# Latent attention with its transposes in groups of eight, and four sets of loads issued at other places

## The chip, the core and the metric

The kernel runs on one core of a Trainium2 chip. A core has five engines that run side by side, each working through its own instructions in the order in which they were written: TensorE (PE in the profile, its weight loads PEld), VectorE (DVE), ScalarE (ACT), GpSimd (POOL) and SyncE (SP), which here issues all the DMAs. They wait for one another through semaphores. Matrix products are written to PSUM, eight banks of 512 float32 columns on 128 partitions; everything else lies in SBUF. The metric is the device time in microseconds of one execution.

## The reference

One layer of an encoder for 1024 tokens of width 1024: a normalisation, one combined input projection, two attention branches, each multiplied by SiLU of its own projection z and projected back, a gated sum of the two, an output projection, the residual and a last normalisation.

```python
proj = h @ w_in          # split into c_q, c_kv, k_rope, z_mla, q/k/v_dil, z_dil, g_mla, g_dil
a_out = mla_attention(c_q, c_kv, k_rope, ...)      # 8 heads, dense softmax over 1024 keys
y_mla = (a_out * silu(z_mla)) @ w_o_mla
d_out = dilated_mixture(q_dil, k_dil, v_dil, positions)   # 3 groups of 8 heads, mixed by softmax denominators
y_dil = (d_out * silu(z_dil)) @ w_o_dil
merged = sigmoid(g_mla + b) * y_mla + sigmoid(g_dil + b) * y_dil
out = rmsnorm(x + merged @ w_out)
```

In one head of the latent attention (`mla_attention`): `s = q @ k.T`, `p = softmax(s)`, `out = p @ v`, with 96 columns of q and k and 64 of v.

## The kernel before, in words

**Precision.** A float32 operand is split into a high part of reduced precision (fp32r, a copy by ScalarE) and a low part (the difference, by VectorE or GpSimd); a product is then three matrix products, high-high, high-low and low-high (`mm3`, lines 145 to 147; `split`, lines 151 and 152). Almost all of the work of TensorE comes from these three lines.

**Order.** The program is written out in full, and each engine executes in the order in which the lines are reached; nothing is reordered. The stages are: the latents and the values of the dilated attention (`first_products`, `first_stage`, to about 205 us), the q and k of the dilated attention and four gates by a scheme with fewer block products (`blocks`), the dilated attention (`attention`), the latent attention (`mla_attention`, about 797 to 1085 us) and the output (`output`). During both attentions a generator, `self.fill`, hands out pieces of another projection whenever `feed` is called: first `gate_fill` (SiLU and gate projections), later `proj_fill` (the two projections back, with the gates).

**The value chunks.** `first_stage` runs 48 chunks `c`, 16 for each of three groups `g` (`r` is the place in the group); a chunk is twelve products of one token tile with one half of the value weights (`v_part`). The weights of a half are loaded by `v_load` in four DMAs into two raw tiles of a pool with two buffers (`w_raw`), and split by `v_split` into four pairs `w_h`, `w_l`: those of the first half of the next group in chunks r = 12 to 14, those of its second half in r = 0 to 2 of that group. The chunks with r = 4 to 7 are the first that use the second half. `block_sums` is a generator whose steps are called once per chunk from c = 30 on, at the end of the chunk: step 1 issues twelve loads (`y`), step 3 scales the first four tiles on ScalarE (line 571), step 4 starts four sums on GpSimd (lines 575 to 578), and later steps split those sums (`parts`, `s_h` on ScalarE and `s_l` on VectorE). `self.table` loads four cosine and sine pieces (`cs_d`) for the stage `blocks`.

**A unit of latent attention.** A unit `k` is one head and two blocks of 128 queries; 32 units run one after another, four ticks `c` each (`mla_tick`). The softmaxed scores P of a unit (128 queries by 1024 keys, twice) have to be transposed for the product with the values: sixteen transposes, four to a tick, written to one of two PSUM banks called `pt` in turn (`mla_transposes`, line 1063). ScalarE copies such a bank to a high part (line 1065), VectorE subtracts to get the low part (`mla_low`, line 1071), and four products with the values follow (`mla_values`, lines 1087 and 1088). They add up in a bank `m_av`, of which there is one; an even unit fills its left half, the odd unit after it the right half. When both are through, in tick 0 of the next even unit, ScalarE copies one part (`mla_copied`, line 1094) and VectorE adds the other (`mla_sum`, line 1103). In ticks 0 and 1 of unit k the scores of unit k + 1 are computed (`mla_scores`), their maxima are taken by VectorE (`mla_maxima`, line 1047) and their exponentials by ScalarE (line 1055). In ticks 2 and 3 `feed` is called. After the last unit of a pair of heads in one half of the queries, `mla_spread` transposes the softmax denominators (line 1117), also into a `pt` bank, and VectorE takes reciprocals (lines 1119, 1120).

The banks and the one accumulator are set here:

```python
b = self.banks
self.places.update(pt=b[0:2], pj=b[2:4], m_av=[])
...
self.places["pj"], self.places["m_av"] = [b[i]], [b[1 - i]]
```

**Loads beside it.** The end of the dilated attention (`combine`, pair 3) is spread over the first ticks of the latent attention: `spread` loads shares of the mixture, `weighted` multiplies by them (line 1636); step 9 comes in tick 15, step 10 in tick 17, step 11 in tick 19. `proj_fill` loads three gate tiles when it begins (tick 34), and its jobs use them in line 1003.

Of the kernel before, what the change touches and what calls it, by code (L numbers as in the profile page):

```python
# [11 lines left out]
F32R = mybir.dt.float32r  # L12
# [37 lines left out]
ZG = (4, 5, 6, 7, 0, 1, 2, 3, *range(16, 24))  # L50
# [11 lines left out]
class Net:  # L62
# [540 lines left out]
    def first_stage(self, cp, dpool, sums):  # L603

        tc, nc = self.tc, self.nc
        self.v_raw, self.v_w, self.v_ps, self.blk, self.opd = {}, {}, {}, {}, {}
        with ExitStack() as ctx, ExitStack() as left, ExitStack() as inner:
            pool = lambda stack, name, bufs=1, **k: stack.enter_context(tc.tile_pool(name=name, reuse_waits="tile", bufs=bufs, **k))
            pl = pool(ctx, "pj_l", 4, space=PSUM)
            pj = pool(ctx, "pj_a", 4, space=PSUM)  # L610
            vp = pool(ctx, "dvp", 3, side="right")
            lp = pool(left, "lp")
            with ExitStack() as stack:
                wl, xp = pool(stack, "wl"), pool(stack, "xp", 3)
                self.first_products(lp, wl, xp, (pj, pl))
            mpool, up, tp = pool(left, "cosm"), pool(left, "up"), pool(left, "lt", 2)
            self.cos_m, self.sin_m = self.table(mpool, "cs_m", 32)
            weights = self.up_weights(up, tp)
            latents = self.latents(next(weights), up, tp, pl)
            self.latent_factors(tp)  # L620
            m = self.masks
            self.mask0 = m[:, 64:320], m[:, 384:640], m[:, 640:896]
            self.mask1 = m[:, 128:384], m[:, 0:256]
            steps, later = 0.0, None
            for c in range(48):
                self.v_part(c, pj, vp)
                g, r = divmod(c, 16)
                if 2 <= c < 10:
                    self.latent_scaled(c - 2)
                if 5 <= c < 8:  # L630
                    next(weights)
                if c == 20:
                    self.token_row(tp, pl)
                first, second = (0, 1) if g & 1 else (1, 0)
                if r == 6:
                    self.v_load(g + 1, first)
                if r == 14:
                    self.v_load(g + 1, second)
                if g < 2 and 12 <= r < 15:
                    for i in ((0, 1), (2,), (3,))[r - 12]:  # L640
                        self.v_split(first, i, nc.gpsimd if g == 0 else nc.vector)
                if g and r < 3:
                    for i in ((0, 1), (2,), (3,))[r]:
                        self.v_split(1 - (g & 1), i, nc.gpsimd if g == 1 else nc.vector)
                if c == 29:
                    self.cos_d, self.sin_d = self.table(dpool, "cs_d", 0)
                if c == 35:
                    self.block_loads(0, self.block_items[0], (self.wp, None))
                if c >= LATENTS_BEGIN and latents:
                    steps += LATENTS_PACE  # L650
                    while steps >= 1 and latents:
                        steps -= 1
                        try:
                            next(latents)
                        except StopIteration:
                            latents = None
                            left.close()
                            sp = pool(sums, "sums")
                            z = self.zero = sp.tile([128, 512], F32, name="zero")
                            nc.gpsimd.memset(z, 0.0)  # L660
                            later = self.block_sums(sp, pool(inner, "bs"))
                elif later and c >= 30:
                    next(later, None)
                if c >= 44:
                    for j in ((0, 1), (2,), (3,), (4,))[c - 44]:
                        self.block_minus(j, self.block_items)
                        self.block_operand(j, self.block_items, nc.vector)
            run_all(later)
            self.block_minus(LEAD, self.block_items)
# [241 lines left out]
    def gate_fill(self):  # L911

        nc = self.nc

        def after(job, i, half, ps):

            z = self.get("zg_g" if 16 <= job < WIDE_END else "zg_z")
            t = self.get("zg_t") if i < 8 else z
            c = slice(half * 512, half * 512 + 512)
            dst = self.zs[i][:, c] if i < 8 else self.gt[i - 8][:, c]  # L920
            yield nc.vector.tensor_tensor(out=z, in0=ps, in1=self.R[:, c], op=ALU.mult)
            if i < 8:
                yield nc.scalar.activation(out=t, in_=z, func=AF.Tanh, scale=0.5)
                nc.gpsimd.tensor_tensor(out=t, in0=t, in1=z, op=ALU.mult)
                nc.gpsimd.tensor_tensor(out=t, in0=t, in1=z, op=ALU.add)
            else:
                yield nc.scalar.activation(out=t, in_=z, func=AF.Tanh, scale=0.5, bias=self.hb[:, i - 8:i - 7])
            stores.append((dst, t))

        def store():  # L930
            if stores:
                self.dma(*stores.pop(0))
        stores = []
        tail = iter(())
        for n, i in enumerate(ZG):
            w = self.split_weights.pop(n)
            for half in range(2):
                next(tail, None)
                ps = self.get("pj")
                t = slice(half * 512, half * 512 + 512)  # L940
                for kc in range(8):
                    self.mm3(ps, *self.at(w, kc), self.hTh[:, kc, t], self.hTl[:, kc, t], kc == 0, kc == 7)
                    if half == 0 and kc == 0:
                        self.weights_load(n + 2)
                    if half == 0 and kc == 4:
                        self.weights_split(n + 1)
                    if kc == 2 or kc == 5 and self.one_bank:
                        store()
                    if kc % 2 and kc < 7:
                        next(tail, None)  # L950
                    if kc < 7:
                        yield
                run_all(tail)
                tail = after(2 * n + half, i, half, ps)
                if self.one_bank:
                    next(tail)
                yield True
        store()
        run_all(tail)
        store()  # L960
        store()

    def proj_fill(self):
# [6 lines left out]
        def gate(n):  # L970
            if n < len(jobs):
                i, dt, half = jobs[n]
                t = self.get("gate")
                self.dma(t, self.gt[8 * i + dt][:, 512 * half:512 * half + 512])
                return t
# [3 lines left out]
        k, pair = 0, (1, 0)  # L979
        for n, (i, dt, half) in enumerate(jobs):  # L980
            while not (self.brd_done if i else self.brm_done[half]):
                yield
            if pair != (i, dt // 2):
                tile, k, pair = tile + 1, 0, (i, dt // 2)
# [72 lines left out]
    def mla_transposes(self, k, c):  # L1057

        pt = self.get("pt")
        for c2 in range(2):  # L1060
            for b in range(2):
                kc, o = 2 * c + c2, c2 * 256 + b * 128
                self.nc.tensor.transpose(pt[:, o:o + 128], self.P[k, b][:, 128 * kc:128 * kc + 128], self.ident)  # L1063
        h, l = self.get("pt_h", dtype=F32R), self.get("pt_l", dtype=F32R)
        self.nc.scalar.copy(out=h, in_=pt)  # L1065
        self.pt[k, c] = pt, h, l

# [82 lines left out]

    def mla_tick(self, k, c):

        self.mla_transposes(k, c)
        if c == 0:
            self.mla_low(k, c)
            self.mla_scores(k + 1, 0)
            self.mla_values(k - 1, 3)
            self.mla_copied(k - 1)
            self.mla_spread(k)
            self.mla_maxima(k + 1, 0)  # L1160
            self.mla_sum(k - 1)
            h, u = self.units[k - 1] if k else (0, 0)
            if u == 3 and h < 6:
                self.mla_load_v(h + 2)
        elif c == 1:
# [7 lines left out]
            if u == 3 and h < 6:  # L1173
                self.mla_load_qk(h + 2)
        else:
            if c == 2:
                self.mla_exponentials(k + 1, 1)
            self.mla_low(k, c)
            self.feed(self.rate)
            self.mla_values(k, c - 1)  # L1180
            if c == 2:
                for n in {6: (), 7: (), 8: (5,), 9: (7,)}.get(k, (k - 1,)):
                    self.mla_merged(n, self.nc.gpsimd)
# [373 lines left out]
    def combine(self, pair, st, nums):  # L1557
# [82 lines left out]
            p.tensor_tensor(out=nums[0][:, c], in0=nums[0][:, c], in1=nums[g][:, c], op=ALU.add)  # L1640

        def step9():
            for half in range(2):
                weighted(0, half, v)
                add(1, half)
            self.turn["bc"] = 1

        def step10():
            spread(2, 0, halves[1])
            weighted(2, 0, v)  # L1650
            add(2, 0)
            self.turn["bc"] = 4
# [247 lines left out]
```

## Time and profile before

| what | us |
|---|---|
| median of 3 runs | 1215.23 (1213.33 to 1217.88) |
| the profiled execution | 1215.87 |
| its span, first to last instruction | 1214.1 |
| TensorE busy in it | 1197.5 |
| VectorE, ScalarE, GpSimd busy | 739.8, 606.1, 557.5 |

The mean granted clock of TensorE was 0.996 of full speed. The 1.8 us between the time of the execution and its span lie before the first and after the last instruction. A busy share close to 100% on TensorE does not mean that each product ran at its best pace, since the products overlap; how far apart two products start is the better measure. In the rows of the timeline the first number is the start, the second the duration, then engine, line, operation, tiles written and read, shapes and count; idle time before it and what ended it stand in brackets. Names such as `at_r` and `at_f` are places in SBUF that many tiles share; `bank`, `left` and `right` are PSUM banks.

### The profile page before, as it was taken

Reading aid. Unit: us, or ns where it says so; the run is one execution under the profiler, and the core shown is the slowest. Engines: PE = TensorE matmul, PEld = TensorE weight load, DVE = VectorE, ACT = ScalarE, POOL = GpSimd, SP = SyncE. Lnnn points to the kernel's source line nnn. Section 1 sums busy time; section 2 is a strip of 40 time slices with the busy share of each in tenths; the row PEclk is TensorE's granted clock in tenths of the full one; section 3 lists DMA queues with packets and bytes.
Section 4 is the critical chain, followed back from the end, with each engine's and each line's share of the span. In section 5 each row is a group of like instructions: output and inputs, shape, how many; then the busy total and the mean of one; then the engine's idle time right before and its main releaser. Section 6 shows DMA issues by size and latency. Waiting matters only on the chain.

```text
span 1214.1 us, 18210 instructions
## 1 busy us (share of the span) xinstructions
PE 1197.5 (99%) x6343; PEld 1030.1 (85%) x6343; DVE 739.8 (61%) x1289; ACT 606.1 (50%) x1259; POOL 557.5 (46%) x473
## 2 busy tenths in 40 slices
PE   9999999999999999999999999999999999999997
PEld 8888878888888888889889899888888888888886
DVE  6775447466666653345666666566757767669442
ACT  6633346343434435356565657454655656654222
POOL 1413027877777777544374624335820111258322
PEclk9999999999999999999999999999999999999999
DMA  8757983597355642397899898937462534235141
GB/s 282 227 192 267 330 311 108 195 281 194 106 139 153 177 122 108 101 289 212 239 258 274 247 263 245 260 107 188 137 171 78 139 105 123 79 121 181 74 154 52
DMA packets 128924, 221.30 MB, mean 182 GB/s; under 512 B 28024, under 2 KB 66496, under 8 KB 123904
## 3 DMA queue, kind: packets, MB, share of 16 engines
q1 hardware_dynamic: 128832, 220.14, 60.5%
q8 instruction: 50, 0.82, 0.3%
q14 instruction: 42, 0.34, 0.1%
HBM read 149.24 MB, written 70.85 MB: 181 GB/s over the span
## 4 chain that ended last, share of the span: by engine, by line
PE 89%; DMA 5%; POOL 2%; DVE 1%; ACT 1%; issue 1%; SPq 0%; POOLq 0%; ACTq 0%; DVEq 0%
PE bank L145 7%; PE bank L146 7%; PE bank L147 7%; PE pj L146 5%; PE pj L147 5%; PE pj L145 5%; PE bank L1063 4%; PE st_d L146 2%; PE st_a L146 2%; PE st_c L146 2%; PE st_c L147 2%; PE st_a L147 2%; PE st_d L147 2%; PE st_d L145 2%; PE st_a L145 2%; PE st_c L145 2%
## 5 line engine op out<-in xcount | busy, mean ns | idle before, releaser
L152 POOL TENSOR_TENSOR w_l<-w_raw,w_h 128x512 fp32r<-128x512 f32 x175 | 230.1, 1327 | 213.2 <-ACT w_h L151 164.5
L151 ACT CAST w_h<-w_raw 128x512 fp32r<-128x512 f32 x188 | 111.7, 620 | 121.7 <-POOL w_raw L684 98.1
L145 PE MATMUL bank<-at_r,w_h 128*128 128x512 f32 x344 | 141.6, 412 | 0.0
L146 PE MATMUL bank<-at_r,w_h 128*128 128x512 f32 x344 | 135.4, 394 | 0.5 <-POOL at_r L152 0.5
L147 PE MATMUL bank<-at_r,w_l 128*128 128x512 f32 x344 | 135.5, 394 | 0.0
L1071 DVE TENSOR_TENSOR at_r<-bank,at_r 128x512 fp32r<-128x512 f32 x128 | 87.9, 687 | 69.0 <-ACT at_r L1065 68.5
L1065 ACT CAST at_r<-bank 128x512 fp32r<-128x512 f32 x128 | 74.9, 585 | 85.4 <-PE bank L1063 84.8
L684 POOL TENSOR_TENSOR w_raw<-w_raw 128x512 f32<-128x512 f32 x64 | 83.2, 1300 | 6.3 <-DVE w_l L152 5.6
L1063 PE MATMUL bank<-consts,at_f 128*128 128x128 f32 x512 | 76.9, 272 | 0.5 <-DVE at_r L1071 0.5
L147 PEld LDWEIGHTS bank<-at_r,w_l 128*128 128x128 f32 x344 | 64.8, 188 | 14.5
L146 PE MATMUL pj<-w_l,at_r 128*128 128x512 f32 x192 | 75.5, 393 | 1.2 <-DVE w_l L152 1.2
L145 PE MATMUL pj<-w_h,at_r 128*128 128x512 f32 x192 | 75.7, 394 | 0.7 <-ACT w_h L151 0.7
L1336 DVE TENSOR_TENSOR at_r<-bank,at_r 128x512 fp32r<-128x512 f32 x64 | 43.9, 685 | 53.0 <-ACT at_r L1332 52.7
L147 PE MATMUL pj<-w_h,at_r 128*128 128x512 f32 x192 | 75.4, 392 | 0.0
L146 PEld LDWEIGHTS bank<-at_r,w_h 128*128 128x128 f32 x344 | 65.2, 189 | 9.7 <-POOL at_r L152 1.0
L145 PEld LDWEIGHTS bank<-at_r,w_h 128*128 128x128 f32 x344 | 65.0, 189 | 8.9
L1088 PE MATMUL bank<-at_r,at_r 128*128 128x256 f32 x256 | 67.2, 284 | 4.2 <-DVE at_r L1071 4.2
L1087 PE MATMUL bank<-at_r,at_r 128*128 128x256 f32 x256 | 67.2, 283 | 0.0
L1317 ACT ACTIVATE at_f<-at_f,at_f 128x256 f32<-128x256 f32 x128 | 64.1, 505 | 1.4 <-DVE at_f L1310 1.4
L1332 ACT CAST at_r<-bank 128x512 fp32r<-128x512 f32 x64 | 37.5, 586 | 54.3 <-PE bank L1324 53.1
L1063 PEld LDWEIGHTS bank<-consts,at_f 128*128 128x128 f32 x512 | 59.3, 140 | 1.3 <-DVE at_r L1071 0.9
L1088 PEld LDWEIGHTS bank<-at_r,at_r 128*128 128x128 f32 x256 | 48.7, 190 | 10.2 <-DVE at_r L1071 5.1
(335 smaller groups left out, 3287.1 us busy)
## 6 DMA issues: line engine op xcount, KB each, us to landing
w_raw<-wt SPq DMA_DIRECT2D x48, 512.0 KB, 4.0
at_r<-s_dq SPq DMA_DIRECT2D x32, 512.0 KB, 8.0
s_dk<-dq_st SPq DMA_DIRECT2D x80, 128.0 KB, 2.3
s_dv<-dv_st SPq DMA_DIRECT2D x16, 512.0 KB, 3.4
s_dq<-dq_st SPq DMA_DIRECT2D x64, 128.0 KB, 2.4
zt<-s_gt SPq DMA_DIRECT2D x32, 256.0 KB, 3.8
w_raw<-wv SPq DMA_DIRECT2D x24, 256.0 KB, 5.7
at_r<-s_dk SPq DMA_DIRECT2D x8, 576.0 KB, 11.8
```

Of the source, the lines that this page charges most:

```text
L145: mm(out, lh, rh, start=start, stop=False, skip_group_check=skip)
L146: mm(out, lh, rl, start=False, stop=False, skip_group_check=skip)
L147: return mm(out, ll, rh, start=False, stop=stop, skip_group_check=skip)
L151: self.nc.scalar.copy(out=h, in_=raw)
L152: sub.tensor_tensor(out=l, in0=raw, in1=h.bitcast(F32), op=ALU.subtract)
L684: self.nc.gpsimd.tensor_tensor(out=b[out], in0=b[x], in1=b[y], op=ALU.subtract)
L1063: self.nc.tensor.transpose(pt[:, o:o + 128], self.P[k, b][:, 128 * kc:128 * kc + 128], self.ident)
L1065: self.nc.scalar.copy(out=h, in_=pt)
L1071: self.nc.vector.tensor_tensor(out=l, in0=pt, in1=h.bitcast(F32), op=ALU.subtract)
L1087: mm(out, vv[:, kc], ph[:, x], start=kc == 0, stop=False)
L1088: mm(out, vv[:, kc], pl[:, x], start=False, stop=kc == 7)
L1317: nc.scalar.activation(out=p, in_=p, func=AF.Exp, scale=-1.0, bias=nm, accum_out=den)
```

## The change

Four things are edited. `mla_transposes` no longer copies; a new function `mla_high` does. Transposes are issued in pairs of groups, eight in a row, in ticks 0 and 2, and the order of copies, low parts, value products and scores within a unit changes with it. The generator of the sums is called from c = 29 on and at the head of a chunk's remaining work, ahead of the loads and splits of value weights; the second half of the last group's value weights is loaded at r = 11 and not at 14, the cosine table at c = 33 and not at 29. The first gate tile of `proj_fill` is loaded by the last job of `gate_fill`. The last share of pair 3 is loaded at the head of step 9 and not in step 10.

```diff
--- before.py
+++ after.py
@@ -632,9 +632,11 @@
                 if c == 20:
                     self.token_row(tp, pl)
                 first, second = (0, 1) if g & 1 else (1, 0)
+                if later and c >= 29:
+                    next(later, None)
                 if r == 6:
                     self.v_load(g + 1, first)
-                if r == 14:
+                if r == (11 if g == 1 else 14):
                     self.v_load(g + 1, second)
                 if g < 2 and 12 <= r < 15:
                     for i in ((0, 1), (2,), (3,))[r - 12]:
@@ -642,7 +644,7 @@
                 if g and r < 3:
                     for i in ((0, 1), (2,), (3,))[r]:
                         self.v_split(1 - (g & 1), i, nc.gpsimd if g == 1 else nc.vector)
-                if c == 29:
+                if c == 33:
                     self.cos_d, self.sin_d = self.table(dpool, "cs_d", 0)
                 if c == 35:
                     self.block_loads(0, self.block_items[0], (self.wp, None))
@@ -659,8 +661,6 @@
                             z = self.zero = sp.tile([128, 512], F32, name="zero")
                             nc.gpsimd.memset(z, 0.0)
                             later = self.block_sums(sp, pool(inner, "bs"))
-                elif later and c >= 30:
-                    next(later, None)
                 if c >= 44:
                     for j in ((0, 1), (2,), (3,), (4,))[c - 44]:
                         self.block_minus(j, self.block_items)
@@ -946,6 +946,9 @@
                         self.weights_split(n + 1)
                     if kc == 2 or kc == 5 and self.one_bank:
                         store()
+                    if kc == 5 and n == len(ZG) - 1 and half:
+                        self.first_gate = self.get("gate")
+                        self.dma(self.first_gate, self.gt[8][:, 0:512])
                     if kc % 2 and kc < 7:
                         next(tail, None)
                     if kc < 7:
@@ -970,6 +973,8 @@
         def gate(n):
             if n < len(jobs):
                 i, dt, half = jobs[n]
+                if n == 0:
+                    return self.first_gate
                 t = self.get("gate")
                 self.dma(t, self.gt[8 * i + dt][:, 512 * half:512 * half + 512])
                 return t
@@ -1061,7 +1066,11 @@
             for b in range(2):
                 kc, o = 2 * c + c2, c2 * 256 + b * 128
                 self.nc.tensor.transpose(pt[:, o:o + 128], self.P[k, b][:, 128 * kc:128 * kc + 128], self.ident)
-        h, l = self.get("pt_h", dtype=F32R), self.get("pt_l", dtype=F32R)
+        self.pt[k, c] = pt
+
+    def mla_high(self, k, c):
+
+        pt, h, l = self.pt[k, c], self.get("pt_h", dtype=F32R), self.get("pt_l", dtype=F32R)
         self.nc.scalar.copy(out=h, in_=pt)
         self.pt[k, c] = pt, h, l
 
@@ -1150,12 +1159,16 @@
 
     def mla_tick(self, k, c):
 
-        self.mla_transposes(k, c)
+        if c % 2 == 0:
+            self.mla_transposes(k, c)
+            self.mla_transposes(k, c + 1)
+            self.mla_high(k, c)
         if c == 0:
             self.mla_low(k, c)
+            self.mla_values(k - 1, 3)
+            self.mla_high(k, 1)
+            self.mla_copied(k - 1)
             self.mla_scores(k + 1, 0)
-            self.mla_values(k - 1, 3)
-            self.mla_copied(k - 1)
             self.mla_spread(k)
             self.mla_maxima(k + 1, 0)
             self.mla_sum(k - 1)
@@ -1173,11 +1186,14 @@
             if u == 3 and h < 6:
                 self.mla_load_qk(h + 2)
         else:
+            self.mla_low(k, c)
             if c == 2:
+                self.mla_values(k, 1)
+                self.mla_high(k, 3)
                 self.mla_exponentials(k + 1, 1)
-            self.mla_low(k, c)
             self.feed(self.rate)
-            self.mla_values(k, c - 1)
+            if c == 3:
+                self.mla_values(k, 2)
             if c == 2:
                 for n in {6: (), 7: (), 8: (5,), 9: (7,)}.get(k, (k - 1,)):
                     self.mla_merged(n, self.nc.gpsimd)
@@ -1640,13 +1656,16 @@
             p.tensor_tensor(out=nums[0][:, c], in0=nums[0][:, c], in1=nums[g][:, c], op=ALU.add)
 
         def step9():
+            if pair == 3:
+                spread(2, 0, halves[1])
             for half in range(2):
                 weighted(0, half, v)
                 add(1, half)
             self.turn["bc"] = 1
 
         def step10():
-            spread(2, 0, halves[1])
+            if pair < 3:
+                spread(2, 0, halves[1])
             weighted(2, 0, v)
             add(2, 0)
             self.turn["bc"] = 4
```

## The prediction

> **What bounds the kernel now.** First the page: busy time of each engine, then the chain of work that ended last.
>
> ```profile
> PE 1197.5 (99%) x6343; PEld 1030.1 (85%) x6343; DVE 739.8 (61%) x1289; ACT 606.1 (50%) x1259; POOL 557.5 (46%) x473
> PE 89%; DMA 5%; POOL 2%; DVE 1%; ACT 1%; issue 1%; SPq 0%; POOLq 0%; ACTq 0%; DVEq 0%
> ```
>
> TensorE has work for 99% of the span and nine tenths of the chain: every microsecond in which it waits is added to the time, and other engines matter only where TensorE waits for them. The places where it waits now stand in the timeline, with the idle time in brackets.
>
> ```profile
> 174.59 0.50 PE L145 MATMUL pj<-w_h,at_r 128*128 128x512 f32 x1 [0.72 <-ACT w_h L151]
> 846.92 0.39 PE L1088 MATMUL bank<-at_r,at_r 128*128 128x256 f32 x1 [1.88 <-DVE at_r L1071]
> 888.76 0.38 PE L1088 MATMUL bank<-at_r,at_r 128*128 128x256 f32 x1 [2.11 <-DVE at_r L1071]
> 162.00:171.00 9.00, 9.00 (x42) 1.00 1.01 314
> 172.00:181.00 9.00, 7.04 (x23) 0.81 1.00 394
> 889.00:893.00 4.00, 4.00 (x18) 0.59 0.80 270
> 893.00:897.00 4.00, 4.00 (x25) 0.98 0.10 37
> ```
>
> The last four are rows by stretch: TensorE's busy time and instructions, its granted clock, DMA. Near 174 us it ran 23 products in nine us instead of 42: 19 × 9/42, about 4.1 us, went there. At 847 it is 1.9 us, 2.2 with the start-up of the next products. At 889 the idle 2.1 us is followed by four us at a clock of 0.59, another 1.7: 3.8 us. The edits of loads aim at these three places, those of the transposes at the 32 units (two query blocks of a head) of latent attention.
>
> **The larger groups of transposes on TensorE.**
>
> ```profile
> 902.30 0.60 PE L1063 MATMUL bank<-consts,at_f 128*128 128x128 f32 x4
> 902.63 0.27 PE L1063 MATMUL bank<-consts,at_f 128*128 128x128 f32 x1
> 902.66 0.48 PE L145 MATMUL bank<-at_r,w_h 128*128 128x512 f32 x1
> 902.98 0.40 PE L146 MATMUL bank<-at_r,w_h 128*128 128x512 f32 x1
> 929.57 0.60 PE L1063 MATMUL bank<-consts,at_f 128*128 128x128 f32 x4
> 929.92 0.47 PE L145 MATMUL right<-at_r 96*128 96x512 f32 x1
> 931.15 0.40 PE L147 MATMUL right<-at_r 96*128 96x512 f32 x1
> 931.38 0.28 PE L1087 MATMUL bank<-at_r,at_r 128*128 128x256 f32 x1
> 931.87 0.60 PE L1063 MATMUL bank<-consts,at_f 128*128 128x128 f32 x4
> 933.71 0.29 PE L1087 MATMUL bank<-at_r,at_r 128*128 128x256 f32 x1
> ```
>
> The first product behind a group takes 0.32 (902.66 to 902.98), where a product of 512 columns takes 0.23 (931.15 to 931.38). That looks like 0.09 for each change of kind, and 64 changes fewer would be 5.8 us. But the last transpose of a group takes only 0.03 (902.63 to 902.66), the three before it 0.11 each (0.33 in three): 0.03 + 0.09 is 0.12, nearly one more transpose. A joined group saves about 0.01: 64 × 0.01, **0.5 us**, with 5.8 as the other end.
>
> **What the new order makes late.** The two PSUM banks for transposes are now filled together, and the sequence at the start of a unit becomes eight transposes, four value products of the unit before, scores, scores, first value products; it was four, scores, four values, four, scores, values. The first value products keep their place on TensorE (the same work lies ahead of them), while the first scores move back by four transposes (4 × 0.11 = 0.44) and four value products (931.38 to 931.87, 0.49): 0.93 us. VectorE works in order, so all behind these scores moves along:
>
> ```profile
> 931.58 1.23 DVE L1047 TENSOR_REDUCE m_nm<-right 128x1 f32<-128x1024 f32 x1
> 932.84 0.68 DVE L1103 TENSOR_TENSOR at_f<-bank,at_f 64x512 f32<-64x512 f32 x1
> 933.55 0.69 DVE L1071 TENSOR_TENSOR at_r<-bank,at_r 128x512 fp32r<-128x512 f32 x1
> 888.02 0.68 DVE L1071 TENSOR_TENSOR at_r<-bank,at_r 128x512 fp32r<-128x512 f32 x1
> L1103 DVE TENSOR_TENSOR at_f<-bank,at_f 64x512 f32<-64x512 f32 x16 | 10.9, 680 | 1.1 <-ACT at_f L1094 0.9
> ```
>
> In an even unit the maximum (L1047) is followed by the sum (L1103), which reads the only accumulator bank, and the next pair's first value product overwrites that bank. The sum ends at 933.52, the value product begins at 933.71: 0.19 to spare. Moved by 0.93 the sum ends at 934.45; 0.06 for the hand-over (888.70 to 888.76) makes 934.51: a wait of **0.8 us**. Sixteen sums less the one after the last unit are 15: **12.0 us**. Bounds by the row: 0.70 if VectorE's pauses close up, 0.86 if they do not, 10.5 to 12.9. The low part (L1071) of the second group, ended at 934.24 + 0.93 + 0.06, or 935.23, must leave its bank before the fourth group; on TensorE that begins after the wait, four values and four transposes: 934.51 + 0.49 + 0.44 = 935.44. No second wait. A plain odd unit has no sum; its low part ends 0.7 sooner, and there I add nothing.
>
> In every second odd unit a transpose of the denominators (L1117) comes between, and takes one of the two banks.
>
> ```profile
> 865.99 0.27 PE L1117 MATMUL bank<-consts,m_den 128*8 128x128 f32 x1
> 866.10 0.60 PE L1063 MATMUL bank<-consts,at_f 128*128 128x128 f32 x4
> 868.40 0.60 PE L1063 MATMUL bank<-consts,at_f 128*128 128x128 f32 x4
> 866.30 0.28 DVE L1119 TENSOR_SCALAR at_f<-bank 8x128 f32<-8x128 f32 x1 [0.67 <-PE bank L1117]
> 868.56 0.66 DVE L1071 TENSOR_TENSOR at_r<-bank,at_r 128x512 fp32r<-128x512 f32 x1
> L1120 DVE RECIPROCAL at_f<-at_f 8x128 f32<-8x128 f32 x8 | 7.5, 941 | 0.3
> ```
>
> From it VectorE needs 3.23 us to the end of that low part (865.99 to 869.22), 3.29 with the hand-over. The third group now writes the very bank which that low part reads. TensorE gets there in 2.41 (865.99 to 868.40) less the group that has moved ahead (0.36): 2.05. The wait is **1.24 us**, seven times (eight reciprocals, the last in the final unit): **8.7 us**, 7.7 to 9.5 by the same pauses. In the final unit no scores cover anything: I add **1.0**, between -1 (its present waits gone) and +2. The copies of both groups (ACT) stay hidden behind the next products, at nothing; if that cover went, they would add their share to the same waits.
>
> **The loads at 174 us.** The edit moves three things ahead: the second half of the value weights (three chunks), the twelve loads of the sums (one chunk, and ahead of the splits), and moves four cosine loads back.
>
> ```profile
> 160.33 0.68 DVE L152 TENSOR_TENSOR w_l<-w_raw,w_h 128x512 fp32r<-128x512 f32 x1
> 161.25 3.57 SPq L141 DMA_DIRECT2D w_raw<-wv  x4
> 164.86 8.80 SPq L141 DMA_DIRECT2D y<-xt  x12
> 171.36 2.67 ACT L571 ACTIVATE y<-y,consts 128x512 f32<-128x512 f32 x4 [0.76 <-DMA y<-xt]
> 174.11 1.27 POOL L575 TENSOR_TENSOR y<-y,y 128x512 f32<-128x512 f32 x1 [52.12 <-ACT y L571]
> 178.06 6.36 DVE L152 TENSOR_TENSOR s_l<-y,s_h 128x512 fp32r<-128x512 f32 x4 [0.44 <-ACT s_h L151]
> ```
>
> The raw weights have two buffers, and both hold the first half until its splits are done, the last at 161.0 (160.33 + 0.68). SP works in order: it can issue the second pair of weight loads only then, and the stores of values and the twelve loads queue behind. So the twelve begin near 163.2 (161.0 and four issues of about 0.5), 1.7 us sooner; without 1 MB of cosines ahead of them I put the first scaling at 168 instead of 171.4. But the scaled rows and their splits now stand **ahead of the last weight split** on ACT and VectorE. From GpSimd's first sum (174.11) to the last of those four subtractions (184.42) it is 10.3 us; beginning at 170.5, and 0.7 later for the weight splits ahead, they end at 181.5, and the last weight part after that, with GpSimd beside it (6.36 in four, 1.6), at 183.1. TensorE wants it at about 174.7 (0.72 of idle before 174.59, then a block of three products and one more). That is 8.4 us of wait and, as after 889, 1.7 of slow clock: 10.1 against 4.1 now, **+6**. If SP is not held, the sums land before 168 and the same queue costs what is lost now: +0. Bounds 0 to +9. Cosine loads and the later SP issues cost nothing: their users start 20 us later.
>
> **The last share and the first gate tile.**
>
> ```profile
> 836.67 1.22 SPq L141 DMA_DIRECT2D at_f<-s_rr  x2
> 845.57 0.69 DVE L1636 TENSOR_TENSOR at_f<-at_f,at_f 128x512 f32<-128x512 f32 x1 [5.07 <-DMA at_f<-s_rr]
> 876.13 0.42 SPq L141 DMA_DIRECT2D at_r<-s_mv  x1
> 887.42 0.69 DVE L1003 SCALAR_TENSOR_TENSOR at_f<-zt,bank 128x512 f32<-128x512 f32 x1 [5.28 <-DMA zt<-s_gt]
> ```
>
> The two share loads go out at 836.67 and are waited for until 845.57; both low parts queue behind that. Two ticks earlier (about 4.5 us) they land near 841 to 843, and TensorE asks at 844.9: **-2.2**. The gate tile now goes ahead of the 512 KB of values (876.13) and a store, only 1.3 us sooner in issue, but with 0.75 MB less before it; at 200 to 330 KB per us that is 2.3 to 3.7, so it is used at 884 to 885 instead of 887.4, with 2.1 needed: **-3.8**. Together -6.0, and -2 if one of them merely shrinks.
>
> **Sum.** On the profiled execution (1215.9, 0.6 above the median of the runs): -0.5 + 12.0 + 8.7 + 1.0 + 6 - 6.0 = +21.2, so 1237.
>
> **A rule against this change.** Waits are short here, but the clock may follow them. After 1.88 us of idling the next products kept their pace, after 2.11 the clock fell to 0.59. In the seven units above, 1.24 of idling is followed at once by eight transposes (0.88): 2.1 us without a product. [...]
>
> **Rivals.** (1) The waits slow the clock: 1249, chance 0.10. (2) **Not slower:** the sum and the low part do not hold TensorE. It decides at the 0.19 us of slack in even units: were the reduction 0.8 us sooner, 20.7 us fall away and 1216 is left. Against it stands VectorE's fixed order; for it, only that no such wait shows today. 0.12, a third of it below 1209, with the sums hidden as well. (3) The change of kind is truly lost time: 5.8 instead of 0.5, 1232; against it the 0.03 row: 0.06. (4) The loads do not come sooner, because the slots hold them: 1243 without the 6.0; 0.06. The forecast has 0.66, by the bounds 1226 to 1247.
>
> **Numbers.** 1224 to 1249 takes in the forecast, (3), (4) and the near half of (1). A measurement here tells about 0.5% from no change. Faster: 0.04, a part of (2). Same: 0.10, the rest of (2) and the forecast's low tail. Slower: 0.86.
>
> **What would show it.** Right: idle tags on L1087 from L1103 in 15 even units near 0.8, on L1063 from L1071 in seven units near 1.2, the last w_l behind four s_l, no tag at the old 847 and 889. Wrong: those tags missing, or granted clock under 0.9 in the latent units.

## The result, and the profile after

The changed kernel takes **1243.7 us** (median of 5 runs, 1242.9 to 1244.5) against 1215.2: 1.0233 of the time before, with a 95% interval of 1.0220 to 1.0245. The forecast was 1237 with a range of 1224 to 1249. The direction and the places were right, but the loss is 28.5 us instead of 21.2.

From the page of the changed kernel, the span, the busy times and the shares of the chain that ended last:

```profile
span 1242.7 us, 18215 instructions
PE 1203.4 (97%) x6343; PEld 1030.8 (83%) x6343; DVE 738.3 (59%) x1289; ACT 610.2 (49%) x1259; POOL 556.2 (45%) x473
PE 85%; DMA 5%; DVE 4%; issue 2%; POOL 2%; SPq 1%; ACT 1%; POOLq 0%; DVEq 0%; ACTq 0%
```

TensorE fell from 99% of the span to 97%, and VectorE's share of the chain rose from 1% to 4%: TensorE now waits for VectorE in places where it did not. Which places, says the view of waits for TensorE (what waited, whom for; us in total, times, longest):

```profile
PE bank L1068 <- DVE at_r L1080: 9.8, 9, 1.4
PE bank L1096 <- DVE at_f L1112: 9.1, 15, 0.7
PE pj L146 <- DVE w_l L152: 7.6, 4, 5.3
PE pj L145 <- ACT w_h L151: 1.6, 1, 1.6
```

In the new file's numbers L1068 are the transposes, L1080 the low parts, L1096 and L1097 the value products, L1112 the sum, L1052 the maximum, L1126 to L1129 the denominators. The same view of before has these rows for L1088 (value products), L1063 (transposes) and L146:

```profile
PE bank L1088 <- DVE at_r L1071: 4.2, 3, 2.1
PE bank L1063 <- DVE at_r L1071: 0.5, 1, 0.5
PE pj L146 <- DVE w_l L152: 1.2, 2, 0.9
```

Of the 4.2 us, 4.0 were the two stalls at 847 and 889. That row is gone; the row of the sum (L1112) is new, and the others have grown.

Where the 28.6 us of span lie follows from three instructions that both kernels have: the first product of the stage behind the value projection, the first transpose of latent attention and its last value product. Their rows, of before and then of after (start in us, duration, TensorE's line):

```profile
209.14 0.39 PE L145 MATMUL st_a<-at_r,w_h 128*128 128x512 f32 x1
797.40 0.60 PE L1063 MATMUL bank<-consts,at_f 128*128 128x128 f32 x4
1087.39 0.28 PE L1088 MATMUL bank<-at_r,at_r 128*128 128x256 f32 x1
```

```profile
218.81 0.39 PE L145 MATMUL st_a<-at_r,w_h 128*128 128x512 f32 x1
807.48 0.71 PE L1068 MATMUL bank<-consts,at_f 128*128 128x128 f32 x5
1115.99 0.28 PE L1097 MATMUL bank<-at_r,at_r 128*128 128x256 f32 x1
```

| stretch | before | after | difference |
|---|---|---|---|
| start to value projection's end | 209.14 | 218.81 | +9.7 |
| to the first transposes | 588.26 | 588.67 | +0.4 |
| latent attention | 289.99 | 308.51 | +18.5 |
| to the end of the span | 126.7 | 126.7 | 0.0 |

Set against the forecast: loads at 174 us 9.7 (forecast 6), latent attention 18.5 (12.0 + 8.7 + 1.0 - 0.5 - 6.0 = 15.2). The first figure is good to about 1 us: order_only and late_loads below, whose code is that of before up to there, come to the same product at 208.67 and 208.07.

### The profile page after: what moved, and what is told of

Read it like the earlier page. It is cut to its first block, busy times and chain, and to the rows that moved or that the text cites. A ratio compares the mean times of both kernels' runs of the same rounds, so it can differ in the third digit from the quotient of the medians.

```text
span 1242.7 us, 18215 instructions
## 1 busy us (share of the span) xinstructions
PE 1203.4 (97%) x6343; PEld 1030.8 (83%) x6343; DVE 738.3 (59%) x1289; ACT 610.2 (49%) x1259; POOL 556.2 (45%) x473
## 4 chain that ended last, share of the span: by engine, by line
PE 85%; DMA 5%; DVE 4%; issue 2%; POOL 2%; SPq 1%; ACT 1%; POOLq 0%; DVEq 0%; ACTq 0%
PE bank L145 7%; PE bank L146 7%; PE bank L147 7%; PE pj L146 5%; PE pj L147 5%; PE pj L145 5%; PE bank L1068 4%; PE st_a L146 2%; PE st_a L145 2%; PE st_a L147 2%; PE st_d L146 2%; PE st_c L146 2%; PE st_d L145 2%; PE st_c L145 2%; PE st_c L147 2%; PE st_d L147 2%
## 5 line engine op out<-in xcount | busy, mean ns | idle before, releaser
L145 PE MATMUL bank<-at_r,w_h 128*128 128x512 f32 x344 | 136.3, 396 | 0.2 <-ACT at_r L151 0.2
L146 PE MATMUL bank<-at_r,w_h 128*128 128x512 f32 x344 | 134.7, 392 | 0.9 <-POOL at_r L152 0.9
L1080 DVE TENSOR_TENSOR at_r<-bank,at_r 128x512 fp32r<-128x512 f32 x128 | 87.1, 685 | 42.0 <-ACT at_r L1074 40.7
L146 PE MATMUL pj<-w_l,at_r 128*128 128x512 f32 x192 | 76.5, 398 | 7.6 <-DVE w_l L152 7.6
L1096 PE MATMUL bank<-at_r,at_r 128*128 128x256 f32 x256 | 73.5, 309 | 9.1 <-DVE at_f L1112 9.1
L1068 PE MATMUL bank<-consts,at_f 128*128 128x128 f32 x512 | 67.8, 275 | 9.8 <-DVE at_r L1080 9.8
L146 PEld LDWEIGHTS bank<-at_r,w_h 128*128 128x128 f32 x344 | 64.9, 189 | 10.8 <-POOL at_r L152 1.2
L1060 ACT ACTIVATE at_f<-right,m_nm 128x1024 f32<-128x1024 f32 x32 | 35.7, 1115 | 67.5 <-DVE m_nm L1052 67.5
L1068 PEld LDWEIGHTS bank<-consts,at_f 128*128 128x128 f32 x512 | 57.6, 141 | 12.1 <-DVE at_r L1080 11.9
L1097 PE MATMUL bank<-at_r,at_r 128*128 128x256 f32 x256 | 66.8, 283 | 0.0
```

What stands on the lines that cost most here:

```text
L145: mm(out, lh, rh, start=start, stop=False, skip_group_check=skip)
L146: mm(out, lh, rl, start=False, stop=False, skip_group_check=skip)
L1080: self.nc.vector.tensor_tensor(out=l, in0=pt, in1=h.bitcast(F32), op=ALU.subtract)
L1096: mm(out, vv[:, kc], ph[:, x], start=kc == 0, stop=False)
L1097: mm(out, vv[:, kc], pl[:, x], start=False, stop=kc == 7)
```

## The experiments

Theory throughout: the waits named in the forecast are the whole loss. The chief rivals were that the cost comes with the grouping itself (two groups of four replaced by one of eight), and, for the loads, that SP held by the two weight buffers is the cause rather than the order of the queues. All ratios are to runs of the kernel before on the same chip.

### One part at a time

Four kernels each keep some edits of the diff and take the rest back: **loads_only** has all four load edits with the old tick, **order_only** the new tick with the old loads, **late_loads** only the last share and the first gate tile, **sums_only** only the edits of the value projection's loop (value weights, sums, cosines).

```
loads_only:  mla_transposes / mla_tick as before; everything else as after
order_only:  mla_transposes / mla_high / mla_tick as after; everything else as before
late_loads:  the first_gate and step9/step10 hunks alone
sums_only:   the hunks at c >= 29, r == 11 and c == 33 alone
```

> All four edits of loads, the order of the units as before. Theory (the order of the units costs about 22, the loads for the sums cost about 10, share and gate tile bring 6): 1215.2 + 9.8 - 6.2 = 1219. Rival (the held SP queue disturbs the later stages too, and the loads carry half of the loss): about 1230.

> The units with groups of eight and their new order, all loads as before. Theory: 15 waits of 0.8, 7 of 1.3 and about 2 more at the end, 1215.2 + 22 = 1237, and the idle times at 847 and 889 remain in some form. Rival as for the loads alone: about 1226 to 1230.

> The last share and the first gate tile sooner, all else as before. Theory: both idle times go, 1215.2 - 6 = 1209. Rival (transfers are only shifted, and the next load is what is late): 1213 to 1215.

> Sums, value weights and cosine table at their new places, all else as before. Theory: the loss near 174 to 192 us as in the changed kernel, 1215.2 + 9.8 = 1225. Rival (it is regained in the next stage, whose operands are ready sooner): 1215 to 1218.

| kernel | median us | before there | ratio, 95% | span |
|---|---|---|---|---|
| loads_only | 1220.1 | 1214.1 | 1.0054 (1.0033 to 1.0074) | 1220.4 |
| order_only | 1237.2 | 1214.1 | 1.0192 (1.0176 to 1.0208) | 1236.2 |
| late_loads | 1210.6 | 1214.1 | 0.9972 (0.9960 to 0.9985) | 1208.4 |
| sums_only | 1224.9 | 1214.1 | 1.0092 (1.0068 to 1.0116) | 1223.5 |

The unit order costs 23.1 us and all loads 6.0; together 29.1, against 28.5 for both at once. The loss at 174 us and the gain at 847 and 889 both belong to the loads: sums_only loses 10.8, late_loads wins 3.5. Each of the four came nearer to the theory's time than to the rival's, late_loads least clearly (1.6 above the one, 2.4 below the other).

The view of waits for TensorE in order_only, whose lines are five lower than in after:

```profile
PE bank L1063 <- DVE at_r L1075: 11.6, 9, 2.1
PE bank L1091 <- DVE at_f L1107: 9.1, 15, 0.7
```

The fifteen waits for the sum are the same 9.1 us as in after. The first row is longer because the late share is still waited for (2.1); the gate tile is not, although its load wasn't touched here. The waits of the units before it have moved the use back, which I take for the reason.

### Putting the sum and the low part first

The forecast's two big terms say that the sum is late because it stands behind the maximum, and that the low part is late because it stands behind the reciprocal and the maximum in VectorE's order. So **sum_first** keeps everything of the change and moves only the sum ahead of the scores and maxima; **low_first** moves only the low part of the second group there; **both_first** does both.

```
 sum_first, in mla_tick, c == 0:
             self.mla_copied(k - 1)
+            self.mla_sum(k - 1)
             self.mla_scores(k + 1, 0)
...
-            self.mla_sum(k - 1)
 low_first, in mla_tick:
             self.mla_high(k, 1)
+            self.mla_low(k, 1)
...
-            self.mla_low(k, c)
```

In low_first the removed line is the one in tick 1.

> The changed kernel with the sum of the accumulator written ahead of the first maximum on VectorE (it needs only the copy that is already done). Theory (the value product waits for that sum, and the sum for the maximum in front of it): the 15 waits go, 1243.7 - 15 x 0.77 = 1232. Rival (the single accumulator bank or the scores' own place is the limit, or the fourth group of transposes waits in its stead): 1239 to 1244.

> The changed kernel with the low part of the second group written ahead of the first maximum. Theory: the seven waits behind the denominators go, the 15 of the sum stay: 1243.7 - 7 x 1.31 = 1234.5. Rival (two banks are too few for groups of eight whatever the order): 1243.

> Both at once. Theory: 1243.7 - 11.6 - 9.2 = 1223, the units at the pace of before. Rival (switching kinds on TensorE costs 0.09 each, so that 64 switches fewer now show): 1223 - 5.3 = 1217.5.

| kernel | median us | ratio to before, 95% | latent attention |
|---|---|---|---|
| after | 1243.7 | 1.0233 (1.0220 to 1.0245) | 308.5 |
| sum_first | 1234.6 | 1.0156 (1.0133 to 1.0179) | 300.4 |
| low_first | 1234.2 | 1.0161 (1.0143 to 1.0179) | 297.5 |
| both_first | 1224.5 | 1.0082 (1.0058 to 1.0106) | 287.7 |

The last column is the stretch of the table above (first transpose to last value product), read in the same way. The waits for TensorE, one fence each for sum_first, low_first and both_first:

```profile
PE bank L1068 <- DVE at_r L1080: 10.6, 10, 1.4
```

```profile
PE bank L1096 <- DVE at_f L1112: 9.1, 15, 0.7
```

```profile
PE bank L1097 <- DVE at_r L1080: 1.5, 3, 1.1
PE bank L1068 <- DVE at_r L1080: 0.9, 2, 0.6
```

Each move removes its own row and leaves the other: sum_first has no row for L1112 left, low_first has none for L1080 among its longest waits. With both, 2.4 us are left of 18.9. The work on VectorE, the groups of eight and the loads are the same in all; only the place in VectorE's queue differs. So the waits are shown to be the queue's order, and grouping by itself is not their cause.

The theory's times were missed by 2.6 us (sum_first), 0.3 and 1.5, the rivals' by more. Ahead of the final unit sum_first wins 8.1 us, less than the 11.5 that its fifteen waits held: most even units are still 0.1 to 0.3 us longer in it than in loads_only, without a wait in the view. low_first wins 8.0 there, and 3.0 more in the final unit; both_first wins 17.8 and 3.0.

Both moves together leave latent attention at 287.7, where the old order with the same loads (loads_only) has 283.9. So the new order is still no gain as a whole. In a unit where nothing waits it is one, of 0.07 us: from its first transpose to that of the next unit, such a unit takes 9.13 us in after (835.19 to 844.32) and 9.20 in loads_only (836.91 to 846.11).

### What makes the loads at 174 us late

**splits_ahead** keeps the change and moves only the step of the sums behind the weight splits of the same chunk:

```
-                if later and c >= 29:
-                    next(later, None)
...
                         self.v_split(1 - (g & 1), i, nc.gpsimd if g == 1 else nc.vector)
+                if later and c >= 29:
+                    next(later, None)
```

> The changed kernel with the step of the sums moved behind the weight splits of its chunk, loads at their new places. Theory (the last weight split queues behind the sums' splits): the loss near 180 us falls from 13.9 to about 5, 1235. Rival (the weight loads come late because SP is held by the two buffers): about 1242.

It takes 1234.1 us, 1.0158 (1.0139 to 1.0176): 9.6 less than after. By the profiles 8.1 of that lie ahead of the next stage, which begins at 210.72 instead of 218.81, and 1.6 in the final unit of latent attention, where the clock stayed at 1.00 (see the rivals below). SP is held in it as in after (the four weight loads take 5.72 us to issue in both), and the sums are asked for at nearly the same time (163.72 and 163.11). VectorE's timeline, first of after, then of splits_ahead (start, duration, and in brackets the idle time ahead):

```profile
172.37 3.06 DVE L152 TENSOR_TENSOR w_l<-w_raw,w_h 128x512 fp32r<-128x512 f32 x2 [4.93 <-ACT w_h L151]
175.86 1.27 DVE L152 TENSOR_TENSOR w_l<-w_raw,w_h 128x512 fp32r<-128x512 f32 x1 [0.43 <-ACT w_h L151]
177.05 6.77 DVE L152 TENSOR_TENSOR s_l<-y,s_h 128x512 fp32r<-128x512 f32 x4
183.74 1.75 DVE L152 TENSOR_TENSOR w_l<-w_raw,w_h 128x512 fp32r<-128x512 f32 x1
```

```profile
172.40 6.47 DVE L152 TENSOR_TENSOR w_l<-w_raw,w_h 128x512 fp32r<-128x512 f32 x4 [4.45 <-ACT w_h L151]
```

The fourth w_l ends at 185.49 in after and at 178.87 in splits_ahead. TensorE waits for it for 5.26 us in the one and 0.74 in the other. By stretch (TensorE's busy time and its instructions, the granted clock, DMA), the windows 172 to 181 and 181 to 190 of after:

```profile
172.00:181.00 9.00, 4.30 (x12) 0.82 1.05 363
181.00:190.00 9.00, 4.46 (x11) 0.50 0.77 203
```

After runs 12 and 11 products where 42 fit: (30 + 31) x 9/42 = 13.1 us, of which the wait for the last w_l is the largest part, with 1.57 of waiting for w_h before it and a clock of half speed behind it. The queue's order, and not the held SP, is thus shown to make most of the loss. What stays in splits_ahead, 18 of 42 products in 172 to 181 (3.9 us), is VectorE at 1.6 us for each w_l, beside GpSimd.

### Two kernels better than either

**best4** is the kernel before with the two late loads, and with the four splits of the second half of the value weights issued in one chunk, before the sums get there. **best** is best4 with the new order of units and both moves of both_first.

```
 best4, in the value projection:
-                    for i in ((0, 1), (2,), (3,))[r]:
+                    for i in ((0, 1), (2,), (3,))[r] if g == 1 else ((0, 1, 2, 3), (), ())[r]:
```

> The kernel before with the last share and the first gate tile sooner, and the four weight splits of the last half all in c = 32, ahead of the scaled rows of the sums; units and all other loads as before. Theory (near 174 us TensorE waits for splits that stand behind the scaled rows, and for VectorE beside GpSimd): 1210.5 - 4 = 1206.5. Rival (the second pair of weight loads lands too late for that, or the sums then come late for the stage behind): 1210 or more.

> The same, with groups of eight and both low part and sum ahead of the first maximum. Theory (a joined group saves 0.01 each, the fixed order still loses about 2 in the units and 2.5 behind them): 1206.5 + 4.5 = 1211. Rival (64 switches at 0.09 each saved): 1202 or less.

best4 takes 1207.4 us, 0.9939 (0.9921 to 0.9958); best takes 1211.0, 0.9958 (0.9942 to 0.9974). Both are faster than before. Their intervals overlap a little, but by the profiles latent attention takes 287.8 us in best and 284.5 in best4, so the new order costs some 3 us even in the best form found. That is not spread evenly: ten units of best are together 5.4 us longer than in best4, the other 21 ahead of the final one 1.8 shorter, the final one 0.3. The first two rows of waits below, 2.7 us, lie in five of the ten; the rest of what makes them longer is open. The time of best met its forecast of 1211, but not by the forecast sum: the stretch behind latent attention, for which 2.5 were added, is 126.7 in both. From VectorE's timeline of best4, and from TensorE's waits of best:

```profile
168.06 1.29 DVE L152 TENSOR_TENSOR w_l<-w_raw,w_h 128x512 fp32r<-128x512 f32 x2 [5.85 <-ACT w_h L151]
169.96 1.29 DVE L152 TENSOR_TENSOR w_l<-w_raw,w_h 128x512 fp32r<-128x512 f32 x2 [0.61 <-ACT w_h L151]
```

```profile
PE bank L1097 <- DVE at_r L1080: 1.4, 3, 0.9
PE bank L1068 <- DVE at_r L1080: 1.3, 2, 1.1
PE bank L1126 <- DVE at_r L1080: 0.5, 1, 0.5
```

In best4 the four w_l are done at 171.25, 0.65 us each, before GpSimd's first sum at 172.99, and the wait at 174 is gone: the next stage starts at 204.05 instead of 209.14.

## Why the prediction was right, and where it was too small

**Even units: 12.0 forecast, 11.5 measured.** Fifteen waits, all on L1096 from L1112. One of them, TensorE and VectorE of after:

```profile
927.19 0.39 PE L147 MATMUL left<-at_r 96*128 96x512 f32 x1
928.13 0.39 PE L1096 MATMUL bank<-at_r,at_r 128*128 128x256 f32 x1 [0.55 <-DVE at_f L1112]
```

```profile
926.26 1.22 DVE L1052 TENSOR_REDUCE m_nm<-right 128x1 f32<-128x1024 f32 x1 [1.00 <-PE right L147]
927.40 0.67 DVE L1112 TENSOR_TENSOR at_f<-bank,at_f 64x512 f32<-64x512 f32 x1
```

Maximum, sum, then the value product 0.06 behind the sum's end: the sequence as forecast. The idle tag reads 0.55, but from start to start it is 0.94 where 0.23 is the pace, so 0.71 are lost, in eight of the units; in the other seven 0.67 idle and 0.83 lost. That the tag is smaller than the loss holds for each of these waits, since the products' modelled ends run past the next one's start. So the tags lie below the 0.8 that was named as the sign, and the fifteen losses still add up to 11.5.

**Denominators: 8.7 forecast, 9.2 measured.** Seven waits on L1068 from L1080:

```profile
936.52 0.28 PE L1097 MATMUL bank<-at_r,at_r 128*128 128x256 f32 x1
937.95 1.09 PE L1068 MATMUL bank<-consts,at_f 128*128 128x128 f32 x8 [1.15 <-DVE at_r L1080]
```

```profile
935.28 0.94 DVE L1129 RECIPROCAL at_f<-at_f 8x128 f32<-8x128 f32 x1
936.15 1.15 DVE L1052 TENSOR_REDUCE m_nm<-right 128x1 f32<-128x1024 f32 x1
937.23 0.66 DVE L1080 TENSOR_TENSOR at_r<-bank,at_r 128x512 fp32r<-128x512 f32 x1
```

1.43 from start to start less the pace of 0.12 is 1.31; 7 x 1.31 = 9.2. Reciprocal, maximum, low part: again the order that was read from the profile of before.

**The joined groups: -0.5 forecast** (64 x 0.01 is 0.6). Eight transposes followed by a product:

```profile
920.13 1.03 PE L1068 MATMUL bank<-consts,at_f 128*128 128x128 f32 x8
920.92 0.37 PE L1096 MATMUL bank<-at_r,at_r 128*128 128x256 f32 x1
```

0.79 us from the first to the product behind them is 7 x 0.109 + 0.03; two groups of four take 2 x 0.36 and one extra start-up of 0.09, or 0.81. So a joined group saves about 0.01 to 0.02, and the rival that the switch is truly lost time (5.8 us) has no support in these rows. The units without waits say the same: they are 0.07 shorter with two joined groups each, where the rival needs 0.18.

**The final unit: +1.0 forecast, +2.7 measured.** This term was too small. From its first transposes to its last value product it took 8.07 us before (1079.32 to 1087.39) and 10.78 after (1105.21 to 1115.99). Its rows, and the window by stretch:

```profile
1107.21 0.27 PE L1126 MATMUL bank<-consts,m_den 128*8 128x128 f32 x1 [0.49 <-DVE at_r L1080]
1109.38 1.74 PE L1068 MATMUL bank<-consts,at_f 128*128 128x128 f32 x8 [1.42 <-DVE at_r L1080]
1108.00:1116.00 8.00, 6.62 (x32) 0.79 0.45 148
```

Two waits, and behind the second the clock falls to 0.79 in the mean of eight us. order_only has the same unit with the same two waits in 9.1 us, at a clock of 1.00, so about 1.6 of the 2.7 is the clock. In low_first the second wait is gone, and the unit takes 7.8.

**Loads at 174 us: +6 forecast, +9.7 measured.** This is the largest part of the error. The path was as forecast: SP held, the twelve loads from 163.11 (163.2), the sums ahead of the last weight part. Sizes failed in three places. GpSimd's first sum came at 171.90, not 170.5; the four s_l took 6.77 and the last w_l 1.75, not 6.36 and 1.6; the last w_l thus ended at 185.49, not 183.1. And the three weight splits before it, for which I had 0.7 in all, ran beside GpSimd (3.06 for two, 1.27 for the third) and held TensorE three more times (7.6 less 5.26, 2.3 us), with 1.6 for w_h. The clock then stayed at half (0.50 from 186 to 191.25), with 0.43 us from start to start, until 191.25:

```profile
185.54 0.80 PE L146 MATMUL pj<-w_l,at_r 128*128 128x512 f32 x1 [5.26 <-DVE w_l L152]
...
191.25 0.51 PE L147 MATMUL pj<-w_h,at_r 128*128 128x512 f32 x1
```

Thirteen products took 5.71 us from start to start where 13 x 0.23 is 3.0: 2.7 us, where I had 1.7. (In loads_only the same wait of 5.3 us is followed by half pace, 0.43 us from start to start, only until 188.57, so some of this differs between executions.)

**Late loads: -6.0 forecast; alone -6.1 in latent attention, here about -3.3.** late_loads has 283.9 for the stretch that takes 290.0 before, and both tags are gone. In the changed kernel less was left to win. Up to the final unit's first transposes latent attention takes 297.7 in after (807.48 to 1105.21) and 301.1 in order_only, a difference of 3.3, which I put down to the waits of the new order: in order_only the gate tile, loaded as before, is no longer waited for.

**Sum.** In latent attention up to the final unit the terms give 11.5 + 9.2 - 6.1 = 14.6 of the 15.8 us by which it grew. At least 0.3 more is a short wait of L1068 for L1080 at 855.44. The rest I cannot place. Of the 7.4 us by which the two profiles differ beyond the forecast, 3.7 are the loads at 174 us, 1.7 the final unit, 1.6 the other units with the late loads (15.8 against 14.2), and 0.4 the stretch between.

**The rivals.** That the waits would slow the clock in the seven units fell: the window over the latent units behind 855 us and ahead of the final one,

```profile
855.00:1105.00 250.00, 232.63 (x1412) 1.00 0.40 114
```

has a granted clock of 1.00 in all, with the waits of 1.15 us, each with eight transposes behind it, in it. The clock under 0.9, named as a sign of being wrong, did come in the final unit, where 0.49 and 1.42 of idling with little between them were followed by 0.79. But the outcome differs between executions: the same two waits were followed by 0.81 in sum_first, and by 1.00 in splits_ahead and in order_only, the second row here. The first row is what came behind order_only's wait of 2.14 for the late share, much as after the 2.11 of before:

```profile
849.00:853.00 4.00, 3.85 (x15) 0.59 0.60 197
1102.00:1110.00 8.00, 6.20 (x39) 1.00 0.33 100
```

The 1249 of this rival needs 12 us more, 7 x 1.7, for a slower clock behind the seven waits. No run shows that term: from 855 to 1105 us, 1.15 us of idling with eight transposes behind it left the clock at 1.00. "Not slower" fell with the 15 and 7 waits. Rival (4), that the share and the gate tile come no sooner, had 1243, near the measured 1243.7, but by chance: in late_loads VectorE uses the share at 843.11 (845.57 before) and the gate tile at 882.41 (887.42), and the stalls are gone in after too. The missing time lay in the loads at 174 us and the final unit.

## What to carry to other kernels

When an order on one engine is changed, look at which instruction of the other engines stands ahead of the one that frees a buffer: here the sum and the low part needed only to be put ahead of the reduction, which gave back 19 us at no cost. Ask what a merged step saves from start to start, not by the displayed pause: two groups of four joined saved 0.01 to 0.02 us by the rows, while the pair needed its buffers back sooner. Work that is asked for earlier is useful only if it goes behind what the bottleneck waits for at that time.

## What was not expected

**Two engines at a time.** VectorE's subtraction takes 0.65 us (1.29 for two, best4) without GpSimd and 1.62 (6.47 for four, splits_ahead) beside it; GpSimd's sums slow as well, here from best4:

```profile
172.99 1.30 POOL L575 TENSOR_TENSOR y<-y,y 128x512 f32<-128x512 f32 x1 [51.96 <-ACT y L571]
177.12 1.62 POOL L578 TENSOR_TENSOR y<-y,y 128x512 f32<-128x512 f32 x1
```

The forecast used this rate for the four s_l and the last w_l, but not for the three w_l ahead of them. One after the other, a subtraction and a sum would take 0.65 + 1.30 = 1.95 us, an estimate from these rows; side by side a pair took about 1.7 (GpSimd's sums in splits_ahead begin at 173.32, 175.00 and 176.70). So in these rows each slows the other, VectorE from 0.65 to 1.62 and GpSimd from 1.30 to 1.62, and side by side they still gain about 0.25 us a pair. Why they slow each other is not shown.

**The scatter between executions.** late_loads removed 6.1 us from latent attention, and 5.6 from one profiled execution to the other (1215.9 to 1210.3), but only 3.5 from the medians. Of the missing 2.0, 1.7 are that the profiled execution of before lies above the median measured beside late_loads, 1214.1. Had I taken that profile's time for the kernel's, I would have overrated the edit by half. The stage ahead of latent attention, which no edit touches, varies too: in the views of waits, TensorE's transposes there waited 2.3 us in loads_only and 1.1 in late_loads (L1329 for L1322), and 0.3 for the same in before (L1324 for L1317). Why is open.

**A recorded clock of 0.95 without loss.** The profile of best4 has a granted clock of 0.948 over the whole span, the others 0.992 to 1.000, and yet it is the fastest. In its window

```profile
172.00:181.00 9.00, 9.00 (x42) 0.95 0.94 365
```

42 products run in nine us, as many as in the window from 162 to 171 before at a recorded 1.00. Here a drop in the record was no loss, for the pace of the products did not fall with it.
